# First modulations on four column groups, early splits on VectorE in order, and two early loads in a two-layer decoder step

## The chip, the cores and the metric

The kernel runs on one core of a Trainium2 chip. The metric is the time of one execution on the device in microseconds, the median of several runs. TensorE (PE in the rows; its weight loads PEld) multiplies matrices into PSUM; VectorE (DVE), ScalarE (ACT) and GpSimd (POOL) do elementwise work; transfers are issued from queues in order, here nearly all from SyncE's (SP). SPq and ACTq are the issuing sides of these queues.

## What is computed

A step of a two-layer decoder for 512 prompt tokens and 8 samples of 8 tokens, 576 columns in all, width 1024. Each layer begins with a modulation of its input and one combined projection:

```python
mod = jax.nn.silu(c) @ w_ada + b_ada          # c: 1 prompt row + 8 sample rows
sh1, sc1, g1, sh2, sc2, g2 = split(mod, 6)
h    = x * (1.0 + sc1) + sh1
proj = h @ w_in                               # retention q, k, v, gate; window q, k, v
# retention + sliding-window attention (bias by distance from a 32-row table)
mix  = concat(ret_out, swa_out) @ w_out
x    = LN1(alpha * x + g1 * mix)              # then conv-FFN with w_up, w_down, and LN2
```

All is float32. Inputs are drawn from a normal distribution; outputs are the two streams, the retention states, the key and value windows and the convolution tails.

## The kernel before, in words

Activations lie transposed: eight tiles of 128 channels x 576 tokens. A product with a weight is done as three matmuls on split operands, high·high, high·low and low·high: a tile is cast to its high part on ScalarE (line 90 for weights, 317 for the first activations), and VectorE or GpSimd subtracts that from the tile for the low part (lines 95 and 318). Weights stream as 512 KB units of eight 128 x 128 tiles through `Weights`: `load` (line 79) issues the transfer into one of two raw buffers, `_emit` (line 83) casts and subtracts, and a raw buffer is free again when both are done. `W.tile(u, j)` prepares two units ahead of the one asked for. Units 0 and 1 are the window's key and value projection, 2 is the first window query (`l0sq0`), 3 and 4 the first retention key and query (`l0r00`, `l0r01`), 5 the first retention value (`l0rv0`).

The first layer starts with nothing prepared. `FirstPart(k0, k1)` (line 329) makes the shift and scale of channel blocks k0 to k1 through `Ada` (line 195): `load` brings rows of `w_ada` (256 KB a transfer; a block of x is 288 KB), `mm(k)` multiplies the 32 columns of silu(c) by them, one column group of 32 for each entry of `begins` (two in `FirstPart`: the shift and the scale), `finish` transposes the result and adds the bias (line 234). The later modulations, of which a stretch runs at each `tick`, use four groups of 512 columns. `start_h(k)` (line 307) makes h of block k and its split; for odd k GpSimd makes the low part. `begin_kv(k)` (line 349) adds block k to the four accumulators of units 0 and 1 (two units x two halves of 288 tokens); in the loop, the low part of a unit's weights is wanted by the third matmul. The order by hand (lines 363 to 408) is: part 0-4, four blocks of x and two weight units loaded, four `start_h`, both weight units split, `begin_kv(0)`, part 4-6 in two halves around `begin_kv(1)`, `begin_kv(2)` and `(3)`, part 6-8 in two halves around `begin_kv(4)`, then `(5)`, the bias row, `(6)` and `(7)`.

TensorE's instructions are pinned to program order; the other engines and the queues take the order that a scheduler plans at build time, except where `keep_in_program_order` puts an instruction behind the one traced before it on its engine. Units 2 and 3 are pinned so.

The bias by distance is one row per head: a matmul and an add make `biasrow` (line 405), SyncE writes it to memory (line 409) and then copies it 128 times there (line 410, `bias_rows`, 1.5 MB), which has to wait for the first trip. Later transfers read it shifted: `l0bias` for the prompt, and in `sample_bias` (line 429) `brow` for the samples, loaded just ahead of 16 small matmuls that spread it over the partitions.

Of the kernel before, what the change touches and what calls it, by code (L numbers as in the profile page):

```python
# [9 lines left out]
F32 = mybir.dt.float32  # L10
# [61 lines left out]
class Weights:  # L72
# [10 lines left out]
    def _emit(self, u):  # L83
        nc, pool = self.nc, self.pool
        if u not in self.raw:
            self.load(u)
        raw = self.raw.pop(u)
        hi = pool.tile([P, 1024], F32R, tag="wh", name=f"wh{u}", bufs=4)
        lo = pool.tile([P, 1024], F32R, tag="wl", name=f"wl{u}", bufs=4)
        cast = nc.scalar.copy(hi, raw)  # L90
        v = u % UNITS
        late = v >= UNITS - 5 or N_IN + 3 <= v < N_IN + N_OUT
        early = v < 3 or N_IN + N_OUT <= v < N_IN + N_OUT + 4
        eng = nc.gpsimd if (early and u != 2) or (v % 3 == 2 and not late and u != 2) else nc.vector
# [26 lines left out]
def _body(ctx, tc, nc, a):  # L121
# [73 lines left out]
    class Ada:  # L195

        def __init__(self, l, begins, nb, tags):
            self.l, self.begins, self.nb, self.tags = l, begins, nb, tags  # L200
            self.nm, self.t, self.acc = f"{l}_{begins[0]}", {}, None

        def load(self, k):
            w, rows = self.nb * P, a["w_ada"][self.l, k * P:(k + 1) * P]
            if len(self.begins) == 2 and w == 256:
                t = unit(self.tags[k % len(self.tags)], f"wa{self.nm}_{k}", w=2 * w)
                o = self.begins[0] * P
                nc.sync.dma_start(out=t.rearrange("p (g c) -> p g c", g=2),
                                  in_=rows.rearrange("p (g c) -> p g c", c=D)[:, 0:2, o:o + w])
                self.t[k, 0], self.t[k, 1] = t[:, 0:w], t[:, w:2 * w]  # L210
                return
            for g, c in enumerate(self.begins):
                t = self.t[k, g] = unit(self.tags[k % len(self.tags)], f"wa{self.nm}_{k}_{c}", w=w)
                nc.sync.dma_start(out=t, in_=rows[:, c * P:c * P + w])

        def mm(self, k):
            if k == 0:
                self.acc = psum("mm" if len(self.begins) == 4 else "tr", f"ada{self.nm}")
            for g in range(len(self.begins)):
# [7 lines left out]
        def finish(self):  # L227
# [4 lines left out]
            trv = tr[:, 0:nb * n].rearrange("p (b g c) -> p b g c", b=nb, g=ng)  # L232
            for g, c in enumerate(self.begins):
                V.tensor_tensor(mods[l][:, c:c + nb, :], trv[:, :, g, 0:9],
                                bc(par[l][:, 32 + c:32 + c + nb], 2, 9), ALU.add)

# [70 lines left out]
    def start_h(k):  # L307
# [9 lines left out]
        S.copy(hi, tmp)  # L317
        (G if k % 2 else V).tensor_tensor(lo, tmp, hi.bitcast(F32), ALU.subtract)

# [30 lines left out]
    def begin_kv(k):  # L350

        for u in range(2):
            wh, wl = W.split(u, k)
            xh, xl = h[k]
            for half in range(2):
                if k == 0:
                    kvps[u][half] = psum("mm", f"l0kv{u}{half}")
                out, o = kvps[u][half][:, 0:HA], half * HA
                T.matmul(out, lhsT=wh, rhs=xh[:, o:o + HA], start=(k == 0), stop=False)
                T.matmul(out, lhsT=wh, rhs=xl[:, o:o + HA], start=False, stop=False)  # L360
                T.matmul(out, lhsT=wl, rhs=xh[:, o:o + HA], start=False, stop=(k == KT - 1))

# [49 lines left out]
    def bias_ap(rows, dims):  # L412
        return bass.AP(scr.tensor, scr.offset + 127, [[8 * 384 - 1, rows]] + dims)

# [13 lines left out]

    def sample_bias():
        sel = unit("S", "sel", w=512)  # L430
        nc.sync.dma_start(out=sel[0:32, :], in_=a["sel"])
        tt = [tok(f"brow{hf}", 544) for hf in range(2)]
        for j in range(2):
            nc.sync.dma_start(out=tt[j][0:32, :].rearrange("p (h k) -> p h k", h=4),
                                in_=bass.AP(scr.tensor, scr.offset + 127 + j * 4 * 384,
                                            [[8 * 384 - 1, 32], [384, 4], [1, 136]]))
            ps = psum("tr", f"biass{j}")
# [128 lines left out]
    def attention(l):  # L566
# [410 lines left out]
        def rest(done):  # L977
# [484 lines left out]
```

## Time and profile before

| | us |
|---|---|
| median of 3 runs | 1491.98 (1489.99 to 1494.51) |
| the profiled execution | 1492.97 |
| its span, first to last instruction | 1491.1 |
| around the span | 1.9 |

TensorE is busy for 97% of the span, VectorE for 56%, ScalarE 42%, GpSimd 32%; its mean granted clock is 0.987 of the full one. In the rows, a time is us from the start of the span, the number after it a duration in us, and a bracket the idle time of the engine before the instruction, with what ended it.

### The profile page before, as it was taken

The numbers are of one execution on the slowest core, as the hardware profiler recorded it, in microseconds if no ns is written. First come the engines' busy times: TensorE is split into PE (matmuls) and PEld (weight loads), VectorE is DVE, ScalarE is ACT, GpSimd is POOL, SyncE is SP. The second block draws the span as 40 slices with busy tenths as digits, with TensorE's granted clock in tenths as the row PEclk, the third lists the DMA queues.
The fourth block names the chain that finished last, engine by engine and source line by source line (L and its number), as shares of the span: only waits on it lengthen the run. The fifth ranks groups of instructions, "written<-read, shape, count | busy, mean of one in ns | idle before, by whom it ended". The sixth has DMA issues, their size and how long they took to land.

```text
span 1491.1 us, 28188 instructions
## 1 busy us (share of the span) xinstructions
PE 1447.6 (97%) x11248; PEld 1359.3 (91%) x11248; DVE 836.4 (56%) x1710; ACT 628.1 (42%) x1282; POOL 477.6 (32%) x646
## 2 busy tenths in 40 slices
PE   6999999999999999999999999999999999999996
PEld 3878889989989999999999889899899999999996
DVE  3257467657654255435566776666675435544565
ACT  2333323348542144325447342334765325523544
POOL 2122212363422132213373312207443213312353
PEclk8999999999999999999999999999999999999999
DMA  9586743333364645332224433332232222222221
GB/s 347 176 262 199 231 140 113 99 123 99 98 225 157 231 157 194 104 90 91 83 71 134 118 94 107 97 98 85 75 100 89 85 81 81 83 86 88 85 61 64
DMA packets 98191, 186.49 MB, mean 125 GB/s; under 512 B 30301, under 2 KB 42765, under 8 KB 97933
## 3 DMA queue, kind: packets, MB, share of 16 engines
q1 hardware_dynamic: 82768, 176.65, 37.6%
q10 hardware_dynamic: 15292, 8.06, 1.9%
q8 instruction: 88, 1.44, 0.4%
q14 instruction: 43, 0.34, 0.1%
HBM read 169.69 MB, written 11.83 MB: 122 GB/s over the span
## 4 chain that ended last, share of the span: by engine, by line
PE 88%; DVE 3%; DMA 3%; ACT 2%; issue 2%; POOL 1%; SPq 0%; ACTq 0%; POOLq 0%; DVEq 0%
PE ada L134 3%; PE l1wo L134 2%; PE l0wo L134 2%; PE l1wdl L134 1%; PE l0wdl L134 1%; DMA wr<-in_wst 1%; PE l1o L134 1%; PE l0o L134 1%; DMA wa<-in_w_ada 1%; POOL wl L95 1%; DMA bias_rows<-bias_row 1%; PE l0kv L134 1%; DVE wl L95 1%; PE l1up2h L134 0%; PE l0up2h L134 0%
## 5 line engine op out<-in xcount | busy, mean ns | idle before, releaser
L90 ACT CAST wh<-wr 128x1024 fp32r<-128x1024 f32 x192 | 200.7, 1048 | 320.1 <-DMA wr<-in_wst 20.1
L95 POOL TENSOR_TENSOR wl<-wr,wh 128x1024 fp32r<-128x1024 f32 x65 | 157.6, 2424 | 433.2 <-ACT wh L90 380.6
L95 DVE TENSOR_TENSOR wl<-wr,wh 128x1024 fp32r<-128x1024 f32 x127 | 160.2, 1262 | 169.8 <-ACT wh L90 151.3
L1172 POOL COPY l0edge<-l0u 128x2 f32<-128x2 f32 x44 | 37.5, 853 | 126.2 <-ACT l0u L1166 126.2
L1180 DVE SCALAR_TENSOR_TENSOR l0c<-l0u,par,l0c 128x592 f32<-128x592 f32 x44 | 48.2, 1098 | 47.2 <-ACT l0c L1179 44.3
L1172 POOL COPY l1edge<-l1u 128x2 f32<-128x2 f32 x44 | 37.6, 854 | 112.7 <-ACT l1u L1166 112.7
L1180 DVE SCALAR_TENSOR_TENSOR l1c<-l1u,par,l1c 128x592 f32<-128x592 f32 x44 | 48.5, 1104 | 44.1 <-ACT l1c L1179 41.3
L134 PE MATMUL ada<-wa,cs 128*32 128x512 f32 (+1 forms) x416 | 58.6, 582 | 5.2 <-DVE cs L184 5.2
L134 PEld LDWEIGHTS ada<-wa,cs 128*32 128x32 f32 x416 | 14.8, 112 | 32.0 <-issue 16.4
L1179 ACT ACTIVATE l1c<-l1u,par 128x592 f32<-128x592 f32 x44 | 38.9, 887 | 3.3
L1179 ACT ACTIVATE l0c<-l0u,par 128x592 f32<-128x592 f32 x44 | 38.9, 887 | 3.3
L1181 DVE SCALAR_TENSOR_TENSOR l1c<-l1u,par,l1c 128x592 f32<-128x592 f32 x44 | 36.6, 834 | 1.4
L1181 DVE SCALAR_TENSOR_TENSOR l0c<-l0u,par,l0c 128x592 f32<-128x592 f32 x44 | 36.6, 834 | 1.4
L481 ACT CAST l0fhi<-l0c 128x512 fp32r<-128x512 f32 (+1 forms) x44 | 16.8, 430 | 46.3 <-DVE l0c L1186 46.3
L481 ACT CAST l1fhi<-l1c 128x512 fp32r<-128x512 f32 (+1 forms) x44 | 16.9, 430 | 37.6 <-DVE l1c L1186 37.6
L796 POOL TENSOR_TENSOR l0sw<-l0sw,c_sin 128x576 f32<-128x576 f32 x8 | 14.3, 1783 | 38.6 <-DMA l0sw<-l0raw 38.6
L796 POOL TENSOR_TENSOR l1sw<-l1sw,c_sin 128x576 f32<-128x576 f32 x8 | 13.0, 1622 | 40.0 <-DMA l1sw<-l1raw 40.0
L482 DVE TENSOR_TENSOR l1flo<-l1c,l1fhi 128x512 fp32r<-128x512 f32 (+1 forms) x44 | 18.2, 454 | 13.0 <-ACT l1fhi L481 13.0
L482 DVE TENSOR_TENSOR l0flo<-l0c,l0fhi 128x512 fp32r<-128x512 f32 (+1 forms) x44 | 18.2, 454 | 12.4 <-ACT l0fhi L481 12.4
L1185 ACT ACTIVATE l1c<-l1c 128x592 f32<-128x592 f32 x22 | 15.4, 698 | 15.0 <-DVE l1c L1181 15.0
L504 POOL TENSOR_TENSOR l1xb<-l1xb,l1ash 128x288 f32<-128x288 f32 x12 | 12.7, 1086 | 25.9 <-issue 25.9
L504 POOL TENSOR_TENSOR l0xb<-l0xb,l0ash 128x288 f32<-128x288 f32 x12 | 12.7, 1087 | 25.9 <-issue 25.9
(3246 smaller groups left out, 5849.0 us busy)
## 6 DMA issues: line engine op xcount, KB each, us to landing
wr<-in_wst SPq DMA_DIRECT2D x192, 512.0 KB, 3.6
wa<-in_w_ada SPq DMA_DIRECT2D x192, 256.0 KB, 5.0
x<-in_xT SPq DMA_DIRECT2D x8, 288.0 KB, 6.2
l0sw<-l0raw SPq DMA_DIRECT2D x32, 72.0 KB, 2.7
l0xb<-in_xT SPq DMA_DIRECT2D x8, 288.0 KB, 3.3
x_spill<-l0x ACTq DMA_DIRECT2D x8, 288.0 KB, 3.2
l1sw<-l1raw SPq DMA_DIRECT2D x32, 72.0 KB, 2.1
l1xb<-x_spill SPq DMA_DIRECT2D x8, 288.0 KB, 3.1
```

The source lines that it names most:

```text
L90: cast = nc.scalar.copy(hi, raw)
L95: sub = eng.tensor_tensor(lo, raw, hi.bitcast(F32), ALU.subtract)
L134: self._add(nc.tensor.matmul(*args, **kw))
L481: S.copy(hi, src)
L482: V.tensor_tensor(lo, src, hi.bitcast(F32), ALU.subtract)
L504: G.tensor_tensor(base[:, o], base[:, o], self.shift[:, o], ALU.subtract)
L796: G.tensor_tensor(sw, sw, sin_t, ALU.mult)
L1172: G.tensor_copy(cm[:, 0:2], t[:, 512:514])
L1179: S.activation(c, t[:, 0:592], AF.Identity, bias=w[3], scale=w[0])
L1180: V.scalar_tensor_tensor(c, t[:, 1:593], w[1], c, ALU.mult, ALU.add)
L1181: V.scalar_tensor_tensor(c, t[:, 2:594], w[2], c, ALU.mult, ALU.add)
L1185: S.activation(ca, ca, AF.Silu)
```

## The change

- `FirstPart` uses a subclass `FirstAda` with four column groups instead of two: shift and scale, each in two halves, so a matmul has half the columns and there are twice as many. The transfers are the same ones. `finish` has half the transposes; its adds join neighbouring groups, for the later modulations all four in one instruction.
- The low parts of weight units 0 and 1, and of all first activations, move from GpSimd to VectorE; the casts and subtractions of units 0 and 1 are pinned, unit 0 behind `start_h(0)`, unit 1 behind `start_h(1)`.
- `begin_kv` runs all four high·high matmuls of both units, then the four high·low, then the four low·high.
- The transfers of units 4 and 5 are issued by hand, 4 between the two trips of the bias row and 5 behind the second.
- The sample bias's transfers are traced about one projection and a half earlier, the matmuls stay where they were.

```diff
-        eng = nc.gpsimd if (early and u != 2) or (v % 3 == 2 and not late and u != 2) else nc.vector
+        eng = nc.gpsimd if u > 3 and (early or (v % 3 == 2 and not late)) else nc.vector
         sub = eng.tensor_tensor(lo, raw, hi.bitcast(F32), ALU.subtract)
-        if u in (2, 3):
+        if u < 4:
             self.tc.keep_in_program_order(cast)
             self.tc.keep_in_program_order(sub)
...
+    class FirstAda(Ada):
+        together = ((0, 2), (2, 4))
+        def __init__(self, k0, k1):
+            h = (k1 - k0) // 2
+            super().__init__(0, (k0, k0 + h, 8 + k0, 8 + k0 + h), h, "M", "tr")
...
-        (G if k % 2 else V).tensor_tensor(lo, tmp, hi.bitcast(F32), ALU.subtract)
+        V.tensor_tensor(lo, tmp, hi.bitcast(F32), ALU.subtract)
...
-            self.ad = Ada(0, (k0, 8 + k0), k1 - k0, "M")
+            self.ad = FirstAda(k0, k1)
...
+        for x in range(3):
+            for u in range(2):
+                for half in range(2):
+                    T.matmul(kvps[u][half][:, 0:HA], lhsT=W.split(u, k)[x == 2], rhs=(xl if x == 1 else xh)[:, o],
+                             start=(k + x == 0), stop=(k == KT - 1 and x == 2))
...
+    for k in range(4):
         start_h(k)
-    W.upto(1)
+        if k < 2:
+            W.upto(k)
...
     nc.sync.dma_start(out=scr1, in_=biasrow[0:8, :])
+    W.load(4)
     nc.sync.dma_start(out=scr, in_=bc(scr1, 0, P))
+    W.load(5)
...
-                    if n == 11 and half == 1 and l == 0:
+                    if (n, half, l) == (10, 1, 0):
+                        sample_bias_rows()
+                    if (n, half, l) == (11, 1, 0):
                         sample_bias()
```

## Rows read from the trace of the kernel before

**Rows 1.** A group of the page: line, engine, operation, count; busy, mean ns; idle

```profile
L95 DVE TENSOR_TENSOR wl<-wr,wh 128x1024 fp32r<-128x1024 f32 x127 | 160.2, 1262 | 169.8 <-ACT wh L90 151.3
```

**Rows 2.** Windows of 1 us: length; PE, PEld, DVE, ACT, POOL; PEclk, DMA, GB/s

```profile
29.00:30.00 1.00, 1.00 (x8) 0.51 (x6) 0.00 (x0) 0.00 (x0) 0.67 (x1) 0.50 1.10 346
64.00:65.00 1.00, 0.17 (x2) 0.00 (x0) 0.00 (x0) 0.52 (x2) 0.00 (x0) 1.00 1.03 397
...
67.00:68.00 1.00, 0.75 (x4) 0.76 (x5) 0.19 (x1) 0.42 (x1) 0.51 (x1) 0.78 0.58 138
...
194.00:195.00 1.00, 0.75 (x8) 0.35 (x8) 0.86 (x6) 0.33 (x1) 0.00 (x0) 1.00 1.07 289
...
197.00:198.00 1.00, 1.00 (x6) 1.00 (x7) 1.00 (x6) 0.00 (x0) 0.00 (x0) 0.64 0.77 294
...
333.00:334.00 1.00, 0.00 (x0) 0.00 (x0) 0.00 (x0) 0.00 (x0) 1.00 (x2) 0.90 0.43 172
```

**Rows 3.** Timeline of the start, all engines, up to the end of part 0-4

```profile
15.38 0.14 PEld L134 LDWEIGHTS ada<-wa,cs 128*32 128x32 f32 x2 [0.54 <-DMA wa<-in_w_ada]
16.46 0.58 ACT L225 COPY adas<-ada 64x512 f32<-64x512 f32 x1 [11.87 <-PE ada L134]
...
17.39 1.04 ACT L90 CAST wh<-wr 128x1024 fp32r<-128x1024 f32 x1 [0.35 <-DMA wr<-in_wst]
```

**Rows 4.** Transfers issued in 12.6 to 12.8 us: KB each, median us to landing

```profile
wr<-in_wst SPq DMA_DIRECT2D x1, 512.0 KB, 6.8
```

**Rows 5.** Timeline, all engines, from the first splits to `begin_kv(0)`

```profile
18.52 2.43 POOL L95 TENSOR_TENSOR wl<-wr,wh 128x1024 fp32r<-128x1024 f32 x1 [16.68 <-ACT wh L90]
18.66 2.36 DVE L315 TENSOR_TENSOR h<-x,st_0s 128x64 f32<-128x64 f32 x1
...
21.32 0.67 ACT L317 CAST h0hi<-h 128x576 fp32r<-128x576 f32 x1 [2.88 <-DVE h L316]
21.66 0.22 DVE L315 TENSOR_TENSOR h<-x,st_0s 128x64 f32<-128x64 f32 x1
...
22.04 0.61 PE L134 MATMUL l0kv<-h0hi,wh 128*128 128x288 f32 x1 [4.42 <-ACT h0hi L317]
22.05 0.75 DVE L318 TENSOR_TENSOR h0lo<-h,h0hi 128x576 fp32r<-128x576 f32 x1
...
26.89 0.61 PE L134 MATMUL l0kv<-h0hi,wl 128*128 128x288 f32 x1 [1.98 <-POOL wl L95]
```

**Rows 6.** Chain that ended last, 0 to 200 us: start, us, what

```profile
28.21 2.75 PE ada L134 x16
...
32.76 1.88 PE ada L134 x16
...
175.87 1.85 PE ada L134 x16
...
181.08 0.69 PE l0os L134 x20
```

**Rows 7.** Timeline of VectorE: low parts of weight units 2 and 3

```profile
48.84 2.75 DVE L95 TENSOR_TENSOR wl<-wr,wh 128x1024 fp32r<-128x1024 f32 x2 [0.31 <-ACT wh L90]
```

**Rows 8.** The chain of rows 6, from 50 us on: bias trips, unit 4, `brow`

```profile
50.28 8.76 DMA bias_rows<-bias_row
...
61.23 3.58 DMA wr<-in_wst
...
67.25 4.71 PE l0r01a L134 x22
...
75.70 3.15 PE l0rv0a L134 x24
...
191.46 4.23 DMA brow<-bias_rows
```

**Rows 9.** The same chain in 186 to 215 us

```profile
195.82 2.88 PE biass L134 x16
198.69 5.82 PE l0rv2b L134 x24
```

More of the change, by code (lines that the diff above doesn't have):

```diff
@@ L195, in _body, with __init__ @@
     class Ada:
-        def __init__(self, l, begins, nb, tags):
-            self.l, self.begins, self.nb, self.tags = l, begins, nb, tags
+        together = ((0, 4),)
+        def __init__(self, l, begins, nb, tags, bank="mm"):
+            self.l, self.begins, self.nb, self.tags, self.bank = l, begins, nb, tags, bank
             self.nm, self.t, self.acc = f"{l}_{begins[0]}", {}, None
@@ L204, in load @@
             w, rows = self.nb * P, a["w_ada"][self.l, k * P:(k + 1) * P]
[L205 to L211, printed above, removed]
             for g, c in enumerate(self.begins):
@@ L217, in mm @@
             if k == 0:
-                self.acc = psum("mm" if len(self.begins) == 4 else "tr", f"ada{self.nm}")
+                self.acc = psum(self.bank, f"ada{self.nm}")
             for g in range(len(self.begins)):
@@ L232, in finish, with load @@
             trv = tr[:, 0:nb * n].rearrange("p (b g c) -> p b g c", b=nb, g=ng)
-            for g, c in enumerate(self.begins):
-                V.tensor_tensor(mods[l][:, c:c + nb, :], trv[:, :, g, 0:9],
-                                bc(par[l][:, 32 + c:32 + c + nb], 2, 9), ALU.add)
+            trv = trv[:, :, :, 0:9].rearrange("p b g c -> p g b c")
+            for g0, g1 in self.together:
+                c, m = self.begins[g0], (g1 - g0) * nb
+                V.tensor_tensor(mods[l][:, c:c + m, :].rearrange("p (g b) c -> p g b c", b=nb), trv[:, g0:g1],
+                                bc(par[l][:, 32 + c:32 + c + m], 2, 9).rearrange("p (g b) c -> p g b c", b=nb), ALU.add)
+    class FirstAda(Ada):
[3 more added lines that the diff above has]
+            super().__init__(0, (k0, k0 + h, 8 + k0, 8 + k0 + h), h, "M", "tr")
+        def load(self, k):
+            w, o, rows = 2 * self.nb * P, self.begins[0] * P, a["w_ada"][0, k * P:(k + 1) * P]
+            if w == 512:
+                t = [unit("M", f"wa{self.nm}_{k}_{x}", w=w) for x in range(2)]
+                for x in range(2):
+                    nc.sync.dma_start(out=t[x], in_=rows[:, x * D + o:x * D + o + w])
+            else:
+                pair = unit("M", f"wa{self.nm}_{k}", w=2 * w)
+                nc.sync.dma_start(out=pair.rearrange("p (g c) -> p g c", g=2),
+                                  in_=rows.rearrange("p (g c) -> p g c", c=D)[:, 0:2, o:o + w])
+                t = [pair[:, 0:w], pair[:, w:2 * w]]
+            for g in range(4):
+                self.t[k, g] = t[g // 2][:, g % 2 * self.nb * P:(g % 2 + 1) * self.nb * P]
     side = []
@@ L350, in begin_kv @@
     def begin_kv(k):
[L352 to L361, printed above, removed]
+        xh, xl = h[k]
+        for x in range(3):
+            for u in range(2):
+                for half in range(2):
+                    if k == 0 and x == 0:
+                        kvps[u][half] = psum("mm", f"l0kv{u}{half}")
+                    o = slice(half * HA, half * HA + HA)
+                    T.matmul(kvps[u][half][:, 0:HA], lhsT=W.split(u, k)[x == 2], rhs=(xl if x == 1 else xh)[:, o],
+                             start=(k + x == 0), stop=(k == KT - 1 and x == 2))
     part = FirstPart(0, 4)
@@ L409, in _body @@
     nc.sync.dma_start(out=scr1, in_=biasrow[0:8, :])
+    W.load(4)
     nc.sync.dma_start(out=scr, in_=bc(scr1, 0, P))
-    def bias_ap(rows, dims):
-        return bass.AP(scr.tensor, scr.offset + 127, [[8 * 384 - 1, rows]] + dims)
+    W.load(5)
     cos_t = const_s("cos", (P, NT))
@@ L427, in _body, with sample_bias_rows @@
     tri = const_s("tri", (P, 256))
-    def sample_bias():
+    sample_rows = []
+    def sample_bias_rows():
         sel = unit("S", "sel", w=512)
@@ L434, in sample_bias @@
             nc.sync.dma_start(out=tt[j][0:32, :].rearrange("p (h k) -> p h k", h=4),
-                                in_=bass.AP(scr.tensor, scr.offset + 127 + j * 4 * 384,
-                                            [[8 * 384 - 1, 32], [384, 4], [1, 136]]))
+                              in_=bass.AP(scr.tensor, scr.offset + 127 + j * 4 * 384,
+                                          [[8 * 384 - 1, 32], [384, 4], [1, 136]]))
+        sample_rows.extend([sel, tt])
+    def sample_bias():
+        sel, tt = sample_rows
+        for j in range(2):
             ps = psum("tr", f"biass{j}")
```

## The prediction

> **What bounds the kernel now.** The page first: TensorE is at work nearly all of the span, so a change pays only where TensorE waits or runs at its lower clock. Then windows of 1 us over the whole span, read for both. [rows 2] shows three places that the change touches: the start, where TensorE is still at 1.2 GHz at 29.5 us; 64 to 68 us, where it ends its work at 64.17 and the clock then falls; and 194.75 to 198 us. The same pattern stands in places that the change does not touch (333 us is one). Then the timeline of the start, engine by engine, to see who makes TensorE wait [rows 3, 5], and the chain of waits, which names a transfer behind each later gap [rows 8, 9]. All sums below are against the profiled execution's 1492.97, which is 1.0 above the median.
>
> **Start, up to the first product.** The last transfer of part 0-4 is used from 15.38, and ScalarE can copy the sums at 16.46 [rows 3]: 1.08 us, most of it two matmul instructions of 512 columns. Four groups of 256 run two by two, so about 0.4 goes; the copy of 0.58 has half the columns, about 0.2 less. VectorE's first h begins 0.6 earlier.
>
> Then [rows 5]: VectorE's small product of line 315 takes 2.36 us while GpSimd subtracts unit 0 (2.43), both ending near 21.0; the same product takes 0.22 three microseconds later. With no split on GpSimd this 2.1 goes. h of block 0 would be ready at 18.66 - 0.6 + 0.22 + 0.22 = 18.5, its high part (0.67) at 19.2, where before it was 22.0. That isn't TensorE's gain: the cast of unit 0, which ran at 17.39 ahead of it [rows 3], is now pinned behind it on ScalarE, and ends at 19.2 + 1.04 = 20.2. So the first matmul moves from 22.04 to 20.2, 1.8 and not 2.8.
>
> The new order wants unit 1's high part for the third matmul. Its transfer lands at 12.64 + 6.8 = 19.4 [rows 4]; ScalarE does the high part of block 1 and this cast after 20.2: 0.67 + 1.04, 21.9. The other ten matmuls of `begin_kv(0)` run at half clock, 0.24 each (5.82 over 24, [rows 9]): 24.3. The low parts must keep up: VectorE has from 18.5 h of block 1 (1.0), two low parts of 0.75 [rows 5] and two of 1.26 [rows 1], 5.0 in all, 23.5; the last two matmuls want theirs at 23.8. In the kernel before TensorE waits 1.98 for GpSimd's unit 1 at 26.89 and is done at 28.2 [rows 5, 6]. Gain **3.8**; if VectorE or ScalarE takes a later block first (1.0 and 0.6), 2.2.
>
> **The column groups.** A half of a later part (4 k, two groups of 256 columns, 16 instructions) takes 1.88 at full clock, and 2 k of four groups of 512 columns take 1.85 [rows 6]. By columns alone a half with 128 would take 0.93; by instructions alone (0.115 each in both rows) its 32 would take 3.7. Between these, the nearest rows: a matmul of 288 columns with its load takes 3.15 / 24 = 0.131 [rows 8], 0.120 of it columns at 2.4 GHz, so 0.011 an instruction; and twenty small ones with their loads take 0.69, 0.035 each [rows 6]. The first gives 0.21 + 8 x 0.011 = 0.30 a k, the second a floor of 0.28: I take 1.15 a half, **0.7** less, and some 2.0 at half clock. Part 4-6: first half 2.75 before, mostly at half clock [rows 2, 6], now 2.0: 0.8 (1.6 if the clock is back). `begin_kv(1)` ran at full clock and may now begin at the lower one: -0.5, between 0 and -1.1. Second half 0.7 (0 at half clock). Part 6-8: 1.4. What is late next is the stream of transfers, in the order of before and saturated (346 GB/s at 29 us, [rows 2]): after unit 1 at 19.4 come two blocks of x and eight transfers of 256 KB, 27.2 by this rate, wanted at about 28.6; the next ten give 35 against some 37. So nothing is lost there, but a gain over about 1.4 more would wait for it. `begin_kv(6)` hangs on h of block 6 as before; the low part of block 7 on VectorE hides behind `begin_kv(6)`, and the joined adds hide behind matmuls.
> Start in all: 3.8 + 0.8 - 0.5 + 0.7 + 1.4 = **6.2**, with bounds 2.2 + 0.8 - 1.1 + 0 + 1.4 = 3.3 and 3.8 + 1.6 + 0.7 + 1.4 = 7.5 (the end at 3.7 a half is a rival, below).
>
> **Unit 4.** TensorE ends `l0r00` at 64.17 [rows 2] and `l0r01`'s first half at 67.25 + 4.71 = 71.96 [rows 8]; such a half takes 3.15 [rows 8], so the gap and the half clock after it cost **4.6**. The cause is SyncE's queue: the second bias trip takes from 50.28 to 59.04, the constants follow, unit 4 goes at 61.23 and lands 3.58 later [rows 8]. In the changed order, with clock times of before (the start's gain moves all of this alike): the transfer waits for a raw buffer, until VectorE has unit 2's low part at about 50.2 [rows 7], 0.75 later with block 7's low part ahead of it. It lands at 54.5, cast and subtraction (1.04, 1.26) end at 57; wanted at 64.2. Behind the waiting load stands the second trip (0.7 later, 1.5 more for unit 4's bytes at 346 GB/s: lands at 61), unit 5 and the constants. Unit 5, should it land only after the trip, is there at 62.5, cast at 63.5 and split on GpSimd (2.43) at 66; wanted when `l0rv0` begins, 75.70 - 4.6 = 71.1. Should the scheduler let the trip go first, unit 4 lands at 60.5 and is split by 62.8: just in time. Bound below: ScalarE keeps the cast of unit 4 behind the copy of `l0r00`'s last half, then some 2 of the 4.6.
>
> **Sample bias.** TensorE ends its work at 194.75 [rows 2], `brow` lands at 195.69 [rows 8], the 16 small matmuls begin at 195.82 [rows 9]: 1.07. The clock falls at 197.28 (0.64 in that window, [rows 2]); `l0rv2b` then takes 5.82 [rows 9] for what costs 3.15 [rows 8], 2.67, and the small matmuls' last 1.41 lose 0.7. In all **4.4**, if the clock stays; 1.1 if it falls without the wait too. The transfers, of 4.23, are traced one projection and a half earlier, some 10 us; in SyncE's queue they pass a weight unit's load, which they delay by the time of their own issue, and they hold two token buffers so much longer, both with units split ahead of need as cover.
>
> Sum: 6.2 + 4.6 + 4.4 = 15.2, so 1477.8 on the profiled execution, 1476.8 on the median; I take **1477**.
>
> **The rivals.** *Unit 4's cast stays late on ScalarE* (the plan puts it behind a copy, so the early transfer is hidden): TensorE still waits, 2.6 of the 4.6 are not gained, 1480. For it: ScalarE's order is planned, not pinned, for unit 4. Against: the cast is traced ahead of that copy. Chance 0.12.
>
> *The clock falls in the small matmuls anyway.* They work on 32 of 128 rows, and before its fall the engine had been idle for 1.07 and then busy with just these for 1.46. Then 3.3 of 4.4 is lost, 1480. Chance 0.12.
>
> *Instructions, not columns, set the time of the groups.* Both forms of [rows 6] cost 0.115 an instruction, so nothing in them excludes that four groups of 128 columns cost the same: a half takes 3.7, four halves 7.3 more than before instead of 2.9 less, 1487. Against it stand the twenty matmuls of [rows 6] at 0.035. Chance 0.05, for this and any milder form.
> The Trainium skill ("TensorE: Matmul & The Clock Gate", Part 3 on the mechanism, and the section on LDWEIGHTS) says that a weight load overlaps a running matmul only where its row group differs, which column groups do not give, and puts a load of 32 columns at 27 ns. By that rule a half would take an estimated 1.7, the four halves gain 0.6 instead of 2.9, and the time is 1479. The trace speaks against it: by it the 2 k of [rows 6] would take 2.1, and they take 1.85.
>
> *The plan is drawn anew, slower.* Only TensorE and four casts are pinned; everything of VectorE, ScalarE, GpSimd and the queues after 20 us is planned again from other start times. A misplaced load or split costs what unit 4's did, 4.6 with the half clock. Four such stalls (18.4 against 15.2) make it no faster than before; with five (23) it is 1500. For it: TensorE idles elsewhere too (333 us, [rows 2]). Against: it is otherwise busy for hundreds of microseconds, and units are split ahead of need. Chance 0.04.
>
> **How the numbers follow.** The forecast, 1477, has 0.67. The bounds of the parts give 3.3 + 2 + 1.1 = 6.4 and 7.5 + 4.6 + 4.4 = 16.5 as gain, 1486 and 1476; a stretch at half clock elsewhere that comes or goes with the shift (3.4, as in the sample bias) reaches to 1472. Range 1471 to 1486, which takes in the first two rivals. A change under 0.3%, 4.5 us, can't be told from none here: faster 0.89, the same 0.06 (parts of the third rival, several parts failing together), slower 0.05.
>
> **What would show it.** Right: no GpSimd split before 30 us and line 315 at 0.2 throughout; first product near 20.2, `begin_kv(0)` done near 24.3; halves of part 4-6 and 6-8 at 1.1; `l0sq0` begun about 6 earlier than before; unit 4's transfer ahead of `bias_rows`, `l0r01a` without a gap; `biass` right behind the window logits, `l0rv2b` at 3.2. Wrong: TensorE waiting for a cast or low part of units 0 and 1 beyond 25 us, for `wa` in part 4-6, for unit 5 or `l0bias` after 56 us, or new gaps after 200 us.

## The result and the profile after

The changed kernel takes 1483.37 us, the median of four runs (1481.32 to 1483.56); the kernel before 1490.99, also of four (1489.06 to 1494.51). The ratio is 0.9934, with a 95% interval of 0.9918 to 0.995. The forecast was 1477, in a range of 1471 to 1486. So sign and range hold, but of a forecast gain of 15.2 us the medians show 7.6 and the profiled executions 9.4 (spans of 1491.1 and 1481.7).

Both traces pass through the same blocks of work in the same order, so the start of a block can be read in both, and the gain at each point is the difference. Of the names that are new here, `l0svt` are transposes behind the first half of `l0r01`, `l0sq1a` and `l0sq2a` begin the second and third window query, and `l0scs` is a small product of the samples between these; a lot of 16 matmuls of the later modulations stands right ahead of `l0sq1a`, another right ahead of `l0sq2a`.

| start of | before | after | gain so far | forecast of this part | measured |
|---|---|---|---|---|---|
| first half of part 4-6 (end of `begin_kv(0)`) | 28.14 | 26.94 | 1.20 | 3.8 | 1.2 |
| `l0sq0a` | 51.30 | 46.90 | 4.40 | 2.4 | 3.2 |
| `l0svt` (behind `l0r01a`) | 71.80 | 63.35 | 8.45 | 4.6 (unit 4) | 4.05 |
| `l0sq1a` | 85.58 | 79.84 | 5.74 | 0 | -2.7 |
| `l0scs` | 96.14 | 89.94 | 6.20 | 0 | 0.5 |
| `l0sq2a` | 118.91 | 113.81 | 5.10 | 0 | -1.1 |
| end of `l0rv2b` | 204.51 | 195.07 | 9.44 | 4.4 (sample bias) | 4.3 |
| end of the span | 1491.1 | 1481.7 | 9.4 | 0 | 0 |

Two parts came nearly as forecast (unit 4 and the sample bias), the first step of the start did not, and waits that the forecast does not have took 3.8 back (2.7 and 1.1). The 0.5 at `l0scs` is a wait of TensorE for VectorE that the kernel before has there and the changed one has not. The rows of each follow.

**Start.** Timeline of the changed kernel, all engines, lines that answer to [rows 5] (line 317 of before is 337 here, 318 is 338):

```profile
19.66 1.04 ACT L90 CAST wh<-wr 128x1024 fp32r<-128x1024 f32 x1
19.79 0.76 DVE L338 TENSOR_TENSOR h0lo<-h,h0hi 128x576 fp32r<-128x576 f32 x1 [0.74 <-ACT h0hi L337]
20.46 0.54 DVE L333 TENSOR_SCALAR h<-x,st_0s,st_0t 128x512 f32<-128x512 f32 x1
20.75 0.85 PE L134 MATMUL l0kv<-h0hi,wh 128*128 128x288 f32 x2 [3.23 <-ACT wh L90]
20.92 1.22 DVE L95 TENSOR_TENSOR wl<-wr,wh 128x1024 fp32r<-128x1024 f32 x1
22.06 0.22 DVE L335 TENSOR_TENSOR h<-x,st_0s 128x64 f32<-128x64 f32 x1
...
22.57 0.67 ACT L337 CAST h0hi<-h 128x576 fp32r<-128x576 f32 x1 [1.87 <-DVE h L336]
...
23.15 1.04 ACT L90 CAST wh<-wr 128x1024 fp32r<-128x1024 f32 x1
...
24.24 0.85 PE L134 MATMUL l0kv<-h0hi,wh 128*128 128x288 f32 x2 [2.63 <-ACT wh L90]
```

The first product runs at 20.75 (forecast 20.2), and line 335 (315 of before) takes 0.22 here. But VectorE puts unit 0's subtraction, 1.22, into the middle of block 1: line 333 is done at 21.0, line 335 begins at 22.06. Block 1's high part on ScalarE waits for that, the cast of unit 1 is held behind it, and TensorE waits 2.63 for this cast. `begin_kv(0)` is done at 26.94, where the forecast has 24.3.

**The column groups.** The tile's own view for part 6-8 of the changed kernel (duration in ns, least, median, most):

```profile
L134 PEld LDWEIGHTS ada<-wa,cs x64: 106/110/110, 36.3 to 39.8; 128*32 128x32 f32 x64
L134 PE MATMUL ada<-wa,cs x64: 272/273/297, 36.3 to 39.9; 128*32 128x128 f32 x64
```

A half, 32 instructions, takes 1.08 here (36.27 to 37.35), where one of 16 with 256 columns took 1.88 [rows 6]; the forecast was 1.15.

**Unit 4.** SyncE's queue in the changed kernel, its issues in order (start, length):

```profile
44.33 0.30 SPq L430 DMA_DIRECT2D bias_row<-biasrow  x1
...
46.26 0.59 SPq L432 DMA_DIRECT2D bias_rows<-bias_row  x1
46.95 2.45 SPq L81 DMA_DIRECT2D wr<-in_wst  x2
49.46 6.46 SPq L441 DMA_DIRECT2D bias_s<-in_mask_s  x4
...
61.80 2.43 SPq L821 DMA_DIRECT2D l0sw<-l0raw  x4
64.33 0.53 SPq L81 DMA_DIRECT2D wr<-in_wst  x1
64.91 0.93 SPq L209 DMA_DIRECT2D wa<-in_w_ada  x2
67.74 2.97 SPq L821 DMA_DIRECT2D l0sw<-l0raw  x4
70.75 2.98 SPq L209 DMA_DIRECT2D wa<-in_w_ada  x6
```

The second trip goes ahead of unit 4 after all. The trace doesn't force this order: VectorE is done with unit 2's low part, and so with the raw buffer, at 46.10, and the trip is issued at 46.26; it is the order of the plan, and why the plan has it isn't shown. The forecast's text has this case, "just in time": behind the trip, unit 4 lands at 57.96, and it is cast and split right when wanted. Timeline of ScalarE, and windows of 1 us in the columns of [rows 2]; the second window holds the wait that is left (0.2 without work, and 0.4 from one matmul's start to the next beyond the usual step), and the clock stays full, where it fell in [rows 2]:

```profile
57.98 1.05 ACT L90 CAST wh<-wr 128x1024 fp32r<-128x1024 f32 x1 [4.07 <-DMA wr<-in_wst]
```

```profile
59.00:60.00 1.00, 1.00 (x9) 0.91 (x7) 0.93 (x1) 1.00 (x3) 0.00 (x0) 1.00 0.16 50
60.00:61.00 1.00, 0.80 (x7) 0.65 (x6) 0.29 (x1) 0.58 (x2) 0.64 (x1) 1.00 0.16 7
```

**What came new.** Two views of the changed kernel: the waits of PEld between 70 and 116 us (total, times, longest), and the first lot of modulations there, 73 to 86 us, by shape (busy us, mean ns). The same shape in the kernel before and two issues of its SyncE queue follow:

```profile
PEld ada L134 <- DMA wa<-in_w_ada: 4.1, 6, 1.0
```

```profile
L134 PE MATMUL ada<-wa,cs 128*32 128x512 f32 x16 | 4.5, 605 | 0.1
```

```profile
L134 PE MATMUL ada<-wa,cs 128*32 128x512 f32 x16 | 1.9, 598 | 0.0
```

```profile
67.75 2.36 SPq L214 DMA_DIRECT2D wa<-in_w_ada  x5
76.17 2.41 SPq L794 DMA_DIRECT2D l0sw<-l0raw  x4
```

These are matmuls of the next modulations, ahead of `l0sq1a`. They want eight transfers of `wa` (pieces of `w_ada`). An `l0sw` is four small transfers that copy a finished projection with its rows exchanged, so its issue waits for ScalarE's copy of that projection out of PSUM. In the changed kernel SyncE's queue issues six of the eight `wa` from 70.75 on, behind the second `l0sw`, which waits for the copy of `l0r01`; TensorE is there at 75.31. In the kernel before six of them are issued ahead of it, one at 62.13 and five from 67.75 on, and TensorE comes at 83.73.

**Sample bias.** The chain of waits of the changed kernel, rows that answer to [rows 9]:

```profile
188.79 0.86 PE l0lg L134 x8
189.65 2.04 PE biass L134 x16
191.69 3.38 PE l0rv2b L134 x24
```

The transfers of `brow` are issued at 175.05, 14.6 ahead of the small matmuls. These have no wait any more, and `l0rv2b` takes 3.38 where it took 5.82.

### The profile page after: what moved, and what is told of

It is laid out like the page before. It is cut to its first block, busy times and chain, and to the rows that moved or that the text cites. A ratio compares the mean times of both kernels' runs of the same rounds, so it can differ in the third digit from the quotient of the medians.

```text
span 1481.7 us, 28349 instructions
## 1 busy us (share of the span) xinstructions
PE 1443.5 (97%) x11340; PEld 1356.5 (92%) x11340; DVE 837.0 (56%) x1701; ACT 627.3 (42%) x1282; POOL 466.9 (32%) x640
## 4 chain that ended last, share of the span: by engine, by line
PE 83%; DVE 3%; ACT 2%; issue 1%; POOL 1%; DMA 1%; SPq 0%; ACTq 0%; POOLq 0%; DVEq 0%
PE ada L134 2%; PE l0wo L134 2%; PE l1wo L134 2%; PE l1wdl L134 2%; PE l0wdl L134 1%; PE l1o L134 1%; PE l0o L134 1%; PE l0up2h L134 0%; PE l1up2h L134 0%; PE l1av L134 0%; PE l1kv0h L134 0%; ACT y L1319 0%; PE l1up3h L134 0%; PE l0up3h L134 0%; DVE wl L95 0%
## 5 line engine op out<-in xcount | busy, mean ns | idle before, releaser
L95 POOL TENSOR_TENSOR wl<-wr,wh 128x1024 fp32r<-128x1024 f32 x63 | 152.9, 2427 | 452.0 <-ACT wh L90 333.1
L134 PE MATMUL ada<-wa,cs 128*32 128x512 f32 (+2 forms) x512 | 58.1, 513 | 6.2 <-DVE cs L184 4.8
L1214 ACT ACTIVATE l0c<-l0c 128x592 f32<-128x592 f32 x22 | 15.4, 698 | 13.3 <-DVE l0c L1210 13.2
```

The costliest lines, as they stand in the source:

```text
L134: self._add(nc.tensor.matmul(*args, **kw))
L1214: S.activation(ca, ca, AF.Silu)
```

## The experiments

None of the twelve kernels leaves anything out of the computation. Theories are named in each expectation. As executions of one kernel differ by several us (e12 shows where), the readings are stages of one trace of each kernel, measured from points inside it. "Start" is the time from the first transposes of the modulations (`adat`) to `l0sq0a`, with "kv0" its first piece, up to the first half of part 4-6; "half clock" is what the granted clock took there (the sum over windows of 0.5 us of 1 minus the clock); then the time from `l0sq0a` to `l0svt`; from the next modulations to `l0sq1a`; and from `l0sq0a` to `l0rv3a`, about 180 us later. The last column is the median of the whole. All in us. Two parts of the change have no run of their own: the new order of `begin_kv`, and unit 5's early load without unit 4's. The kernel before, run beside e1 to e4, e5 to e8 and e9 to e12, had medians of 1492.93, 1493.87 and 1493.78; the two medians at the head of the table are those of the first comparison.

| kernel | kv0 | start | half clock | to `l0svt` | modulations | to `l0rv3a` | median |
|---|---|---|---|---|---|---|---|
| before | 10.95 | 34.11 | 5.1 | 20.50 | 1.85 | 183.19 | 1490.99 |
| changed | 9.83 | 29.79 | 5.1 | 16.45 | 4.53 | 177.85 | 1483.37 |
| e12, changed again | 9.82 | 28.43 | 3.4 | 16.51 | 4.34 | 177.78 | 1482.37 |
| e1 | 7.85 | 27.72 | 3.4 | 16.97 | 4.95 | 178.60 | 1483.31 |
| e2 | 9.63 | 28.54 | 3.4 | 16.48 | 4.81 | 177.58 | 1481.72 |
| e3 | 9.84 | 32.14 | 3.4 | 16.00 | 2.92 | 175.91 | 1484.09 |
| e4 | 9.81 | 29.43 | 5.1 | 16.00 | 5.01 | 178.40 | 1479.69 |
| e5 | 9.82 | 28.76 | 3.4 | 16.04 | 2.28 | 177.11 | 1482.08 |
| e6 | 7.84 | 26.77 | 3.4 | 15.99 | 2.76 | 176.32 | 1482.03 |
| e7 | 9.82 | 28.94 | 5.1 | 16.49 | 4.83 | 180.50 | 1482.48 |
| e8 | 11.85 | 32.25 | 6.8 | 17.37 | 5.11 | 179.19 | 1486.48 |
| e9 | 9.82 | 29.19 | 5.1 | 23.02 | 1.86 | 182.70 | 1486.46 |
| e10 | 7.84 | 28.68 | 5.1 | 16.77 | 1.86 | 176.44 | 1478.01 |
| e11 | 7.84 | 26.86 | 3.4 | 15.99 | 1.85 | 173.65 | 1478.24 |

### The start

**e1: casts of units 0 and 1 not held in order**

```diff
-        if u < 4:
+        if u in (2, 3):
```

> The casts and subtractions of units 0 and 1 are no longer held in program order, so ScalarE casts unit 1 ahead of block 1's high part. In the changed kernel this cast runs at 23.15 to 24.19 and TensorE waits 2.63 us for it at 24.24. Theory A (the order on ScalarE and VectorE is what kept the start's gain at 4.4 of the forecast 6.2): the cast runs at about 20.7 to 21.8, begin_kv(0) ends at about 24.5 where it ended at 26.9, and part 4-6 begins there; l0sq0 begins up to 2.4 earlier than 46.90, and the run gains 0 to 2.4 on 1483.4, by what the later modulations' wait swallows. Rival B (the stream of transfers is the bound): begin_kv(0) ends early, but part 4-6 waits for its wa until about 26.7, l0sq0 begins within 0.5 of 46.90, and the time stays.

Timeline of ScalarE and TensorE in this run:

```profile
19.35 1.99 ACT L90 CAST wh<-wr 128x1024 fp32r<-128x1024 f32 x2
22.26 0.67 ACT L337 CAST h0hi<-h 128x576 fp32r<-128x576 f32 x1 [0.92 <-DVE h L336]
```

```profile
21.39 0.85 PE L134 MATMUL l0kv<-h0hi,wh 128*128 128x288 f32 x2 [0.42 <-ACT wh L90]
```

Both casts run back to back, the wait of 2.63 is 0.42, and part 4-6 begins at 24.65 (expected 24.5). Theory A: kv0 is 1.97 shorter, here and in the three other runs with this edit. That is most of the 2.6 by which this step missed its forecast. The transfers did not hold part 4-6 back, rival B falls. How much of the 1.97 is kept varies. `l0sq0a` is 2.38 earlier than in the changed kernel's first profile, but that one ran longer at half clock (5.1 against 3.4). Against e12, the changed kernel with 3.4 as well, it is 0.8 earlier: the clock came back at 28.0 here and at 27.2 there, so that the first half of part 4-6 and `begin_kv(1)` take 4.31 here and 3.05 there. The rest goes up to `l0svt` and at the wait for `wa` (`l0sq1a` at 78.39): `l0rv3a` begins at 223.12, in e12 at 223.08, and the median of four runs (1482.14 to 1484.60) shows no gain. With the `wa` earlier in both (e6 against e5, each 3.4) the start keeps the whole 2.0.

**e2: block 1 ahead of unit 0**

```diff
     for k in range(4):
         start_h(k)
-        if k < 2:
-            W.upto(k)
+        if k == 1:
+            W.upto(1)
```

> Unit 0's cast and subtraction are placed behind block 1's in program order, still held: ScalarE does the high parts of blocks 0 and 1 first, then units 0 and 1; VectorE does block 1 in one piece ahead of unit 0's subtraction. In the changed kernel VectorE puts unit 0's subtraction (20.92, 1.22 us) into the middle of block 1. Theory A (the cost was that subtraction in the middle of block 1, and the cast of unit 1 behind it): block 1's h is ready at about 21.3, its high part at 22.0, the casts of units 0 and 1 at about 21.5 to 23.1 at the latest; the first matmul comes about 0.7 later than 20.75, but begin_kv(0) ends at about 25.3 instead of 26.9, and l0sq0 up to 1.5 earlier. Rival B (transfers bound part 4-6, about 26.7): l0sq0 within 0.5 of 46.90.

Block 1 is in one piece and its high part begins at 20.96, but the two casts come behind it, 21.54 to 23.53, and the first product at 22.63 instead of 20.75. kv0 is 0.2 shorter, not 1.5: theory A misses. So it isn't the subtraction in the middle of block 1 by itself that costs, it is that the casts stand behind block 1's high part at all.

**e3: two column groups again, same transfers**

```diff
-        together = ((0, 2), (2, 4))
+        together = ((0, 1), (1, 2))
...
-            super().__init__(0, (k0, k0 + h, 8 + k0, 8 + k0 + h), h, "M", "tr")
+            super().__init__(0, (k0, 8 + k0), k1 - k0, "M", "tr")
```

> The first modulations go back to two column groups (256 columns in parts 4-6 and 6-8) with the transfers of the changed kernel. Theory A (columns, not instructions, set their time): a half at full clock goes from the changed kernel's 1.08 back to about 1.88, one at half clock from 1.94 to about 2.8; l0sq0 begins 2.9 to 3.3 later than 46.90, and the time rises by up to that on 1483.4 (less by what the later modulations' wait, 3.35 in the changed kernel, gives back). Rival B (at the start the stream of transfers or VectorE is the bound, so the halves' time is hidden): l0sq0 begins within 1 of 46.90 and the time stays within 1.

The three halves at full clock take 1.92 each (1.08 with four groups); the shape's row, 26.5 to 44 us, its first half partly at the lower clock:

```profile
L134 PE MATMUL ada<-wa,cs 128*32 128x256 f32 x64 | 7.9, 391 | 0.0
```

The start is 3.7 longer than in e12 and 2.4 longer than in the first profile, so this time was not hidden: theory A. What the later wait gives back is seen too: the modulations take 2.92 instead of 4.53, and the median is 0.7 above the changed kernel's, not 3.

**e8: subtractions of units 0 and 1 and of the odd blocks on GpSimd, as before**

```diff
-        eng = nc.gpsimd if u > 3 and (early or (v % 3 == 2 and not late)) else nc.vector
+        eng = nc.gpsimd if u < 2 or (u > 3 and (early or (v % 3 == 2 and not late))) else nc.vector
...
-        V.tensor_tensor(lo, tmp, hi.bitcast(F32), ALU.subtract)
+        (G if k % 2 else V).tensor_tensor(lo, tmp, hi.bitcast(F32), ALU.subtract)
```

> Subtractions of units 0 and 1 and of the odd blocks go back to GpSimd. Theory A (VectorE's line 335 took 2.36 us because GpSimd was at work beside it): line 335 of block 1 takes 2 us or more again, its high part ends at about 24, the cast of unit 1 at about 25.3, unit 1's subtraction on GpSimd (2.43) at about 27.8, and begin_kv(0) ends at about 28.4 instead of 26.9; l0sq0 begins 1.4 or more later. Rival B (GpSimd costs only its own longer subtractions, and VectorE loses the one in the middle of block 1): line 335 stays at 0.22, the cast of unit 1 ends at about 23.3, and begin_kv(0) ends at about 26.3, 0.6 earlier than in the changed kernel.

Timeline of VectorE and GpSimd in this run:

```profile
20.44 2.37 DVE L335 TENSOR_TENSOR h<-x,st_0s 128x64 f32<-128x64 f32 x1
```

```profile
20.31 2.42 POOL L95 TENSOR_TENSOR wl<-wr,wh 128x1024 fp32r<-128x1024 f32 x1 [18.47 <-ACT wh L90]
```

Line 335 takes 2.37 again and ends with GpSimd's subtraction, 22.8 and 22.7; kv0 is 2.0 longer and part 4-6 begins at 28.49 (expected 28.4). Theory A. The Trainium skill ("SBUF — State Buffer", "Who interferes with whom") says that a VectorE instruction with two inputs in SBUF contends with a GpSimd instruction that reads SBUF, over a shared pair of ports that acts as an exclusive lock; these two rows agree.

### Unit 4 and the modulations behind it

**e4: the constants ahead of the bias row's first trip**

```diff
     W.load(3)
+    cos_t = const_s("cos", (P, NT))
+    sin_t = const_s("sin", (P, NT))
...
+    tri = const_s("tri", (P, 256))
     begin_kv(2)
...
     W.load(5)
-    cos_t = const_s("cos", (P, NT))
-    sin_t = const_s("sin", (P, NT))
...
-    tri = const_s("tri", (P, 256))
```

(in short: the loads of constants behind `W.load(5)`, twelve in the kernel, are moved up to behind `W.load(3)`, nothing else)

> The fifteen loads of constants behind the bias row's second trip are put ahead of its first trip, into the 8 us in which SyncE's queue waited for the bias row; behind them stand the first trip, units 4 and 5, the second trip. Theory A (the later modulations waited for wa because SyncE's queue stood behind the second trip: 4.5 us, and all constants behind that): the second half of l0's mask loads to wa go some 5 us earlier, the modulations before sq1a (4.61 us for 16 matmuls in the changed kernel, 1.92 in the kernel before) and before sq2a (3.27) run without a wait, and the time falls by 2.7 to 3.8 to about 1480. Unit 4 lands well ahead of need. Rival B (wa waits for its buffers or for the plan's place, not for the queue's head): the modulations still wait, and the time stays at 1483.4.

Units 4 and 5 go ahead of the second trip, and no constant waits behind it any more: from 51.6 to 59.17 the queue stands at the first `l0sw`, which waits for the copy of `l0r00`. The last 0.45 at unit 4 goes (16.00). But the modulations take 5.01: theory A falls. The queue's head was not the trip. It was the second `l0sw`, which waits for the copy of `l0r01` whatever stood ahead, with six `wa` behind it (69.57 in this run). The median, 1479.69, is the "about 1480" of theory A, but without its mechanism: the profiled execution took 1485.08 and shows the wait, and what made the others short isn't known.

**e5: the first `wa` one item earlier**

```diff
-                (it_kq, (0, 1), [], [v_rows]),
-                (it_v, (0,), [tick], [lg(0, 0)]),
+                (it_kq, (0, 1), [tick], [v_rows]),
+                (it_v, (0,), [], [lg(0, 0)]),
```

> The first two k of l0's second modulations are loaded one item earlier in program order (ahead of l0r01, not ahead of l0rv0a); the matmuls on them stay where they are. Theory C (the loads of wa stood in SyncE's queue behind the l0sw that waits for l0r01's copy, and this, not the bias row's second trip, is why the modulations wait): all eight wa are issued right behind l0r00's l0sw, at about 64.3 to 68, and land by about 73; the modulations ahead of sq1a take 1.92 instead of 4.60, sq1a begins at about 77.1 instead of 79.84, and the time falls by about 2.7 to 1480.7; those ahead of sq2a (3.27) stay or gain 1.1 more. Rival B (bandwidth: the queues carry 300 to 390 GB/s there): eight loads earlier push unit 6 and the l0sw back, l0rv0a or the modulations still wait, and the time stays within 1 of 1483.4.

SyncE's queue, and the waits of PEld between 70 and 116 us, in this run:

```profile
61.95 3.93 SPq L209 DMA_DIRECT2D wa<-in_w_ada  x8
65.97 0.55 SPq L81 DMA_DIRECT2D wr<-in_wst  x1
66.61 3.17 SPq L821 DMA_DIRECT2D l0sw<-l0raw  x4
```

```profile
PEld ada L134 <- DMA wa<-in_w_ada: 2.0, 4, 1.0
PEld l0sq1a L134 <- ACT wh L90: 1.3, 1, 1.3
PEld l0sq1a L134 <- DVE wl L95: 1.0, 1, 1.0
```

Theory C: all eight go ahead of the second `l0sw`, and the matmuls ahead of `l0sq1a` wait for no transfer any more (2.28 for 4.53, of which 0.36 is the next wait). A piece of rival B is there too: unit 6's load now stands behind eight transfers, and `l0sq1a` waits for its cast and low part, which loses 1.1 again. The wait that is left, 2.0, is the lot ahead of `l0sq2a`. The median, 1482.08, shows 1.3 of the 2.7 expected.

**e6: e1 and e5 together**

> Both edits: units 0 and 1 not held in program order, and the first wa loads one item earlier. Theory (the two losses are apart, and the start's gain was swallowed by the wait for wa alone): l0sq0 at about 44.5, no wait for wa ahead of sq1a, sq1a at about 74.8 instead of 79.84; 2.1 + 2.7 = 4.8 less than the changed kernel, about 1478.6, the forecast's 1477 within 2. Rival (wa lands at about 78.4 whatever stands ahead, as in the four runs so far: sq1a began at 78.39, 78.42, 78.65 and 80.51): sq1a not before 78, and the time within 1.5 of 1483.4.

`l0sq0a` at 43.39 and `l0sq1a` at 74.08: it does not stay at 78.4, so the rival falls, and up to `l0rv3a` the kernel is 5.0 ahead of the first profile of the changed one and 3.4 ahead of e12. The median shows 1.3 and 0.3 of that; the profiled execution lost 8.5 to the lower clock after 230 us, more than any other.

**e9: no early load of units 4 and 5**

```diff
-    W.load(4)
     nc.sync.dma_start(out=scr, in_=bc(scr1, 0, P))
-    W.load(5)
```

> The two early loads of units 4 and 5 go; they are loaded where their use asks for them. Theory C (the stall at unit 4 and the wait for wa are two ends of one budget: l0r01's copy, and with it the l0sw and the wa behind it, comes 4.2 earlier in the changed kernel): unit 4 is issued behind the constants at about 57 to 61, TensorE waits for it about 3 and then runs at half clock, l0svt begins 3.5 to 4.5 later than 63.35; but the modulations ahead of sq1a lose their wait (1.92 instead of 4.60), sq1a begins only 0.7 to 1.5 later than 79.84, and the time is about 1 more, 1484.4. Rival (the early load is worth its full 4.2): sq1a 4 later than 79.84, 1487.6.

Timeline of TensorE, and two windows, in this run:

```profile
62.10 0.40 PE L134 MATMUL l0r01a<-h0hi,wh 128*128 128x288 f32 x1 [3.35 <-ACT wh L90]
```

```profile
61.00:62.00 1.00, 0.00 (x0) 0.00 (x0) 0.00 (x0) 1.00 (x1) 0.00 (x0) 1.00 1.00 376
...
64.00:65.00 1.00, 1.00 (x6) 1.00 (x6) 0.76 (x1) 0.14 (x1) 0.78 (x1) 0.50 0.31 98
```

The wait at unit 4 is back, with the half clock behind it: 6.6 up to `l0svt` (expected 3.5 to 4.5). The modulations need no wait then, 1.86 as expected: as in the kernel before, six `wa` are issued ahead of the second `l0sw` (from 63.71, the `l0sw` at 73.56). Up to `l0sq1a` 4.3 is lost, as the rival has it, and up to `l0rv3a` 4.9. So the early load is worth more than the 4.05 read from the first comparison, and theory C's claim that the two losses nearly cancel falls. What holds of it is that the wait for `wa` ahead of `l0sq1a` is there where the stall at unit 4 has gone, and not where it stands.

**e10: e1, and the `wa` ahead of `l0r01`'s second half**

```diff
-                (it_kq, (0, 1), [], [v_rows]),
-                (it_v, (0,), [tick], [lg(0, 0)]),
+                (it_kq, (0, 1), [], [tick, v_rows]),
+                (it_v, (0,), [], [lg(0, 0)]),
```

> Units 0 and 1 not held in order, and the first wa loads put ahead of l0r01's second half, behind unit 6's load. With the wa loads ahead of its first half, 1.1 was lost again at the second use of unit 6 (sq1a waited 1.3 for its cast and 1.0 for its low part). Theory: unit 6 lands first, this wait goes, the modulations ahead of sq1a run without a wait, sq1a about 5.8 earlier than in the changed kernel (74.0) and l0scs too (84.1); 5.5 to 6 less up to 230 us. On the whole time about 1478, give or take the stretches at half clock after 300 us, of which the runs so far show two to four, 3.4 to 8.5 us in all. Rival: the wa now land too late again, sq1a at 76 or later.

Unit 6 is issued ahead of the eight `wa`, and both waits ahead of `l0sq1a` are gone (1.86, and 10.21 from there to `l0scs` where e5 had 11.20). `l0sq1a` begins at 75.76, not 74.0, since this execution had 5.1 of half clock at the start.

**e11: e4 and e10 together**

> As the run before, and the constants ahead of the bias row's first trip. Theory: unit 4 lands about 5 earlier than it is wanted, its remaining 0.4 of wait goes, l0svt about 4.0 earlier than 63.35 with the start's 2.1 and more; in all 6 less than the changed kernel up to 230 us, about 1477.5 with the same stretches at half clock behind. Rival: the second trip, now behind units 4 and 5, lets the window bias or the sinks come late, and a new wait of 1 or more appears between 60 and 85 us.

Of the waits for `wa` between 70 and 116 us 0.2 is left (4.1 in the changed kernel), the 0.45 at unit 4 is gone, and no new one of 1 us shows up to `l0rv3a`. That stretch takes 173.65, 4.1 less than in e12 and 4.2 less than in the changed kernel: of these 4.2, 2.7 are ahead of `l0sq1a`, 1.3 ahead of `l0sq2a`, 0.45 at unit 4, less 0.25 lost in smaller pieces. The 1.3 ahead of `l0sq2a` goes in neither e4 nor e10, only in both together; what held these transfers is open. With the start, `l0rv3a` begins at 217.71 against 223.08 in e12.

**e12: the changed kernel again**

> The changed kernel once more, on the chip of the three others: 1483.4 within 1.5 by every theory; its landmarks up to 230 us within 1 of the first profile's, and the difference between executions in the stretches at half clock after 300 us.

Windows of 1 us in this execution, and the second of them in the first profile:

```profile
27.00:28.00 1.00, 1.00 (x33) 0.79 (x25) 0.00 (x0) 0.00 (x0) 0.00 (x0) 0.86 1.08 361
28.00:29.00 1.00, 1.00 (x12) 1.00 (x9) 0.00 (x0) 0.00 (x0) 0.00 (x0) 1.00 1.11 352
```

```profile
28.00:29.00 1.00, 1.00 (x20) 0.59 (x10) 0.00 (x0) 0.00 (x0) 0.00 (x0) 0.50 1.10 352
```

The same instructions, kv0 alike to 0.01, but the clock is back at 27 us and not at 30.5: 1.4 of the start, and more than the 1 allowed. `l0sq0a` begins at 45.30, 6.0 earlier than in the kernel before, where the first profile has 4.4; so a total of the start hangs on the execution, and kv0 does not. Between 230 and 1460 us windows of 2 us at less than 0.97 stand at up to three places (318 to 342, 822 to 832, 1036 to 1062 us); what they lose (2 us times 1 minus the clock, summed) is 5.1 before, 6.8 in the changed kernel, and 1.7 to 8.5 in the other runs. A gain of 1 to 4 us can go under in that. From `l0rv3a` to the end the fourteen traces take 1253.7 to 1260.5 us; with the clock's loss over that stretch taken off, 1246.4 to 1248.9.

On this chip, with six runs each, e10 has 1478.01 and e11 1478.24 where the changed kernel has 1482.37; against the kernel before the ratios are 0.9901 (0.9882 to 0.9921), 0.99 (0.9882 to 0.9917) and 0.9926 (0.9908 to 0.9943). The changed kernel is thus 11.4 us faster by these medians, where the first comparison has 7.6. e10 and e11 have some 4 us less again by the medians, which the traces up to 225 us bear out for e11; the intervals still overlap. For e10 the stretch from `l0sq0a` on gains 1.3 and kv0 2.0, while its profile had the longer half clock at the start.

### Sample bias

**e7: `brow` loaded at its use**

```diff
-                    if (n, half, l) == (10, 1, 0):
-                        sample_bias_rows()
                     if (n, half, l) == (11, 1, 0):
+                        sample_bias_rows()
                         sample_bias()
```

> The loads of sel and brow go back to their use, the rest stays as changed. Theory A (the wait of 1.07 and the half clock behind it are the 4.35 us of this part): the small matmuls wait about 1, the clock falls behind them, l0rv2b takes 5.5 to 5.8 instead of 3.38, and the run takes 4.4 more, about 1487.8. Rival B (the clock stayed full because the work ahead of it came at another time): the wait returns and the clock stays, 1.1 more.

The chain of waits in this run:

```profile
185.88 3.97 DMA brow<-bias_rows
...
189.98 2.09 PE biass L134 x16
192.07 4.90 PE l0rv2b L134 x24
```

The wait is back, 0.81 on TensorE, and the clock falls behind it (0.50 from 193 to 195 us): theory A by its mechanism, rival B falls. The price is 2.4 and not 4.4, because the clock came back at 196; in [rows 9] `l0rv2b` ran 0.9 longer still, and the small matmuls 0.8. The loss by the half clock is thus known only within this factor. The median of two runs, 1482.48, shows none of it.

## Why the prediction was right, and where not

**First product, line 335, GpSimd** (start): right. 20.75 against 20.2, 0.22 throughout, and e8 puts a price of 2.0 on it.

**`begin_kv(0)` done at 24.3**: wrong by 2.6, the largest error of the start. The step that failed is "ScalarE does the high part of block 1 and this cast after 20.2: 0.67 + 1.04, 21.9". It takes block 1 as ready by 20.2. VectorE first waits 0.74 for block 0's high part and takes its low part (0.76), so that even in one piece block 1 is ready only at 20.9 (e2); with unit 0's subtraction in its middle it was ready at 22.5. ScalarE does its high part then, and unit 1's cast behind it ends at 24.2 instead of 21.9. VectorE's sum of 5.0 was right as a sum and said nothing about its order. The text's own lower bound, 2.2, was above the 1.2 that came: it allowed for a later block in between, not for a weight unit. That the cast was held behind block 1 cost 1.97 (e1), and without this part 4-6 begins at 24.65.

**The groups**: right. 1.08 against 1.15, and e3 shows that this time isn't hidden. The rival by instructions (3.7 a half) falls. The rule of the Trainium skill quoted in the prediction ("TensorE: Matmul & The Clock Gate", Part 3, "The mechanism": a load overlaps a running matmul only in another row group) would have given an estimated 1.7; the row decides against it here. `begin_kv(1)` at the lower clock cost 0.8 (forecast 0.5, bound 1.1), and nothing in the second execution. The stream of transfers, named as late next, did not become the bound: in e1 part 4-6 ran 2.3 earlier and did not wait. The rest of the start gained 0.8 over its forecast: two of the four halves are followed by the copy and the transposes of `finish`, and with these each gained 1.1, not 0.7.

**Unit 4**: right, 4.05 for 4.6, by the weaker of its two cases (the trip first, with 0.45 left of the wait). What kept unit 4 behind the trip in the kernel before is more than the order of the queue: a constant in between had to wait for the trip's semaphore (last section). The rival with a late cast falls: the cast stands ahead of the copy, at 57.98.

**What was late next behind unit 4**: missing from the sum, which puts it at nothing: 3.8 lost, 3.3 with the 0.5 that came at `l0scs`. The step that failed follows SyncE's queue past the trip, unit 5 and the constants, and stops there; its signs of being wrong name `wa` only in part 4-6. It takes the later modulations, whose row it uses for a price, as matmuls with no transfers of their own to be late. In the kernel before five of the `wa` were issued from 67.75 on, when `l0r01` had just begun; with the stall at unit 4 gone the plan puts the `l0sw` of `l0r01` ahead of six, and TensorE arrives 8.4 earlier. That this order costs the 2.7 ahead of `l0sq1a` is shown by e5 and e10, which load the `wa` earlier, and by e9, where the stall is back and the old order with it; for the 1.1 ahead of `l0sq2a` the cause is open. This is the "plan is drawn anew" rival in a mild form: one loss near the forecast's price for a misplaced load (4.6), where the rival has a chance of 0.04 for four of them at once. One such should have stood in the sum's bounds.

**Sample bias**: right, 4.3 for 4.4, and the clock did not fall in the small matmuls: that rival (1480) falls in the changed kernel and in all eleven runs with `brow` ahead. How much of the 4.3 is a matter of the execution is open: with the wait back e7 loses 2.4.

**Sum**: 1.2 + 3.2 + 4.05 + 4.3 - 3.3 = 9.45 against 15.2. The difference of 5.75 is 2.6 of `begin_kv(0)`, 3.3 of the wait for `wa`, 0.55 of unit 4 and 0.1 of the sample bias, less the 0.8 that the rest of the start gained over its forecast. In e12, with the shorter half clock at the start, the gain at the end of `l0rv2b` is 11.1. That the time lies in the range is partly luck: the lower bound, a gain of 6.4, has 2.2 for `begin_kv(0)` and nothing for a wait for `wa`, and it held because unit 4 and the sample bias came nearly in full, not at the 2 and 1.1 of that bound.

## What to carry to other kernels

A stall that is removed brings forward the work of the engine that stood still, and not the transfers that this work wants: list for the next 20 us which transfers TensorE then wants, and behind which waiting issue each of them stands. When a cast or a subtraction is held in program order, its time is that of the last instruction ahead of it, so follow the producer's order instruction by instruction and not by its sum. And compare kernels by stages inside the trace, at like time at the lower clock: here kv0 repeated within 0.03 us in the executions of a like order, while the whole start moved by 1.4 in one and the same kernel and four to six whole runs spread over 2 to 9.

## What the runs showed of the hardware

One and the same instruction stream got its clock back at 27 us in one execution and at 30.5 in another, and each lost 6.8 us to the lower clock after 230 us, at two places in one and at three in the other. Over the runs, whose edits all lie in the first 200 us, that loss is 1.7 to 8.5. The scatter of the stretch behind `l0rv3a`, 6.8 us over the fourteen traces, is 2.5 without that loss.

What looks like a queue that is held up by a long transfer is here a wait of the program's own. In the changed kernel the issue of the masks stood 4.5 us with nothing of its own to wait for; in the kernel before the constants stood 5.2 us so, and unit 4 behind them. The changed queue's waits in 43 to 62 us:

```profile
SPq L441 <- DMA bias_rows<-bias_row: 4.5, 1, 4.5
SPq L346 <- DMA o_kv<-l0kv: 2.5, 2, 1.8
```

The trace's records name the semaphores. Each transfer signals its landing by one of eight (100, 102 to 105, 107 to 109), which the program gives out in turn to the transfers of SyncE and ScalarE alike, and an issue waits until the one that had its semaphore before has landed: in both traces each of the 436 issues for which that landing is recorded comes behind it. The bias trip has 105 and lands at 55.57; the fourth mask is the next with 105 and is issued at 55.59. The two constants of the second line have the semaphores of the two outputs `o_kv`, which ScalarE issued at 48.12 and 48.95. So a transfer that takes long holds up the issue that is given its semaphore next, and all that stands behind that issue. What more semaphores would change was not tried.
